# A hybrid decoder step on one core: the recurrence's pace, a later decode update, z through the weight landing buffers, and VectorE in order of tracing

## The chip, the cores and the metric

The kernel runs on one core of a Trainium2 chip. A core has five engines that work at the same time and meet through semaphores: TensorE (PE, matrix products), VectorE (DVE, elementwise work and reductions), ScalarE (ACT, functions and copies), GpSimd (POOL) and SyncE (SP, which issues most transfers). Each works through its own instructions in the order in which the program holds them. The metric is the time of one execution in microseconds on the device; lower is better.

## The reference

One inference step of two layers: a causal Conformer convolution and an RWKV-7 time-mixing layer, each followed by a squared-ReLU MLP, for 1040 prompt tokens (16 of them learned) and 8 decode rows, all in float32, width 1024, 16 heads of 64. The part that the change touches is the second layer's mixer and what follows it:

```python
def _wkv7_step(S, inp):
    r_t, w_t, k_t, v_t, kk_t, a_t = inp
    sa = jnp.einsum('bhvk,bhk->bhv', S, -kk_t)
    S = (S * w_t[:, :, None, :] + sa[..., None] * (kk_t * a_t)[:, :, None, :]
         + v_t[..., None] * k_t[:, :, None, :])
    y = jnp.einsum('bhvk,bhk->bhv', S, r_t)
    return S, y
...
    kk = kk / jnp.maximum(jnp.sqrt(jnp.sum(kk * kk, axis=-1, keepdims=True)), L2_EPS)
...
    S_final, ys = lax.scan(_wkv7_step, S0.astype(f32), xs)
...
    out = ((yn + bonus).astype(h.dtype) * g) @ w_o
...
def _sqrelu_mlp(h, w_in, w_out):
    return jnp.square(jax.nn.relu(h @ w_in)) @ w_out
```

The prompt's scan over 1040 tokens starts from zero; the 8 decode rows make one step from a given state.

## The kernel before

Everything is held with features on the 128 partitions and tokens along the free dimension. Products that need full accuracy are made of three fast ones: a weight block is split into a high part (ACT, L156) and a low part (POOL in four pieces, L161), the activations likewise (`split`, L137), and `mm3` (L186 to L188) adds up high*high, low*high and high*low.

**Stages.** The first layer runs to about 1120 us and isn't touched. Then come four mixer groups of 272, 256, 256 and 264 tokens (`mixer_in(g)`), then the output projection and the second MLP, first for the first third of the tokens (`mixer_out(0)` and `mlp`), then for the other two thirds together.

**Mixer group.** `prepare(g)` loads the input rows and makes differences and mixed inputs on DVE. `keys(g)` makes the eight key projections, keeps them, and sums their squares over heads in the PSUM tile `pn`; at its end stand the norm's reciprocal root `r16` and its split (L889 to L895). `mixer_in(g)` then goes through eight pairs of heads: projections r and v, the low-rank gate and decay, on DVE the normalised key (L1061, which needs `r16` through `spread`), a scan of the decay (L1062), and products into `ab`. `finish` of a pair is delayed by one pair: it writes `ab`, the transposed values and a block of products `n` to DRAM (L1009 to L1021). During pair p the keys of group g + 1 are made. The last pair's finish is `carry["tail"]`, run at the start of the next group, and behind the loop for the last one.

**Recurrence.** The scan is done in 17 chunks: chunk 0 of the 16 learned tokens, then 16 of 64. Per chunk the inverse of a triangular matrix is needed: `inverses` loads the blocks `n` of a group's four chunks back from DRAM (L1135) and eliminates row by row in 30 steps of two DVE operations (L1141, L1142), eight operations to a piece, and writes the result `d_p`. `front(c)` loads a chunk's operands and makes the products A, `chunk(c)` goes through the products gg, bT, W, po, U, S and Y, with a copy or an elementwise step on DVE or ACT between any two of them. Both are generators; each `yield` gives a weight from `RW` (sum 27.72), meant as the distance to the next step. `chunk` also calls `step(c + 1)` three times, which moves the next chunk's front on by one yield without its weight being charged; this happens only once that chunk's inverse is there.

**Ticks.** `tick(g)` is called at the start of a pair and twice within each projection: it moves the inverses by one yield, adds `PACE[g]` to a credit from which the recurrence's steps are paid (a credit that nothing could be paid from is lost), and moves the norms of the first token group (`ng0`: load y, head norms, write z to DRAM) by one yield. In the MLP, `filler` is called 208 times in the first group and spreads three streams over the calls in proportion: the rest of the recurrence, the decode rows' step (`decode_step`: eight transposes on PE, a round trip through DRAM, then 16 rounds of nine DVE operations on the state, L1375 to L1383) and the norms of the other tokens.

**Order.** A planner puts each engine's instructions in an order by its own simulation, priorities following the order of tracing. Within `in_order()` PE's instructions keep the order of tracing exactly; DVE, ACT, POOL and SP are the planner's. A tile's memory may be reused by tiles of a later pool; then each new tile waits for the old tiles that lie in its place. The pools of the mixers (input rows, differences, narrow weights, mixed inputs, low-rank tiles, pair tiles, in this order) are followed in the same place by those of the MLP: temporaries, statistics, activations, split weights, and so on.

**Output projection.** `mixer_out(g)` loads z through the temporaries `t1` (three buffers), splits it into `z`, and per block of 128 output features loads and splits the weights and multiplies (`dense`).

## Time and profile before

| | us |
|---|---|
| median of 3 runs | 2803.23 (2798.64 to 2806.42) |
| profiled execution, its own time | 2803.45 |
| its span, first to last instruction | 2801.7 |
| PE busy | 2654.4 (95%) |
| DVE busy | 1772.9 (63%) |
| POOL busy | 1497.7 (53%) |
| ACT busy | 1141.9 (41%) |

The span is read in stages: an engine's share of the whole span is a mean over stages with different limits. Busy times are read per window, waits by who released them, and the timeline instruction by instruction. In a timeline row stand start, duration, engine, line of the kernel, operation, output and inputs, count, and in brackets the idle time of that engine just before, with what ended it. PE's row of weight loads is called PEld; it runs beside the products.

### The profile page before, as it was taken

The numbers are of one execution on the slowest core, as the hardware profiler recorded it, in microseconds if no ns is written. First come the engines' busy times: TensorE is split into PE (matmuls) and PEld (weight loads), VectorE is DVE, ScalarE is ACT, GpSimd is POOL, SyncE is SP. The second block draws the span as 40 slices with busy tenths as digits, with TensorE's granted clock in tenths as the row PEclk, the third lists the DMA queues.
The fourth block names the chain that finished last, engine by engine and source line by source line (L and its number), as shares of the span: only waits on it lengthen the run. The fifth ranks groups of instructions, "written<-read, shape, count | busy, mean of one in ns | idle before, by whom it ended". The sixth has DMA issues, their size and how long they took to land. (4 is left out here: it accounts for less than half of the span.)

```text
span 2801.7 us, 51779 instructions
## 1 busy us (share of the span) xinstructions
PE 2654.4 (95%) x19866; PEld 2502.9 (89%) x19866; DVE 1772.9 (63%) x3550; ACT 1141.9 (41%) x2101; POOL 1497.7 (53%) x2066
## 2 busy tenths in 40 slices
PE   8998999999999999999998999978999999999998
PEld 7998999999999999787777778767889999999998
DVE  5999999996454544244756555589985554434444
ACT  5545444543354333233343443444444452222223
POOL 6676877887788866022111112366568763333332
PEclk9998999999999999999999999989999999999999
DMA  6663544454445553567778767877775642222211
GB/s 179 176 178 89 160 136 134 135 177 136 138 138 159 170 149 95 163 192 196 188 175 203 184 162 188 190 201 187 181 212 160 179 122 81 71 72 69 68 53 42
DMA packets 624599, 412.31 MB, mean 147 GB/s; under 512 B 121865, under 2 KB 567497, under 8 KB 624351
## 3 DMA queue, kind: packets, MB, share of 16 engines
q1 hardware_dynamic: 543436, 358.60, 45.1%
q10 hardware_dynamic: 72386, 24.56, 4.2%
q0 software_dynamic: 8528, 25.83, 2.8%
q8 instruction: 157, 2.57, 0.4%
q14 instruction: 92, 0.75, 0.1%
HBM read 345.76 MB, written 64.07 MB: 146 GB/s over the span
## 5 line engine op out<-in xcount | busy, mean ns | idle before, releaser
L161 POOL TENSOR_TENSOR wo_lo<-wo_raw,wo_hi 128x256 fp32r<-128x256 f32 x736 | 564.3, 798 | 261.0 <-ACT wo_hi L156 250.2
L161 POOL TENSOR_TENSOR wi_lo<-wi_raw,wi_hi 128x256 fp32r<-128x256 f32 x640 | 488.2, 794 | 282.7 <-ACT wi_hi L156 268.1
L186 PE MATMUL out<-hh,wo_hi 128*128 128x352 f32 (+2 forms) x1536 | 503.5, 328 | 21.5 <-DVE h L354 10.9
L354 DVE TENSOR_TENSOR h<-h,out 128x352 f32<-128x352 f32 (+2 forms) x768 | 387.5, 510 | 200.2 <-PE out L188 199.6
L188 PE MATMUL out<-hl,wo_hi 128*128 128x352 f32 (+2 forms) x1536 | 494.3, 324 | 5.5 <-DVE hl L140 5.5
L188 PE MATMUL ps_in<-m_l,wi_hi 128*128 128x352 f32 (+2 forms) x1536 | 495.5, 323 | 2.7 <-DVE m_l L284 2.6
L186 PE MATMUL ps_in<-m_h,wi_hi 128*128 128x352 f32 (+2 forms) x1536 | 496.4, 323 | 1.2 <-DVE h L354 1.2
L187 PE MATMUL out<-hh,wo_lo 128*128 128x352 f32 (+2 forms) x1536 | 495.8, 323 | 0.0
L187 PE MATMUL ps_in<-m_h,wi_lo 128*128 128x352 f32 (+2 forms) x1536 | 492.6, 321 | 0.0
L518 DVE SCALAR_TENSOR_TENSOR cv<-u,wdw,cv 128x352 f32<-128x352 f32 (+2 forms) x720 | 376.3, 571 | 0.7
L156 ACT CAST wi_hi<-wi_raw 128x1024 fp32r<-128x1024 f32 x160 | 168.0, 1050 | 399.9 <-PE out L188 195.8
L156 ACT CAST wo_hi<-wo_raw 128x1024 fp32r<-128x1024 f32 x184 | 192.6, 1049 | 320.0 <-PE out L188 159.0
L186 PEld LDWEIGHTS out<-hh,wo_hi 128*128 128x128 f32 x1536 | 293.1, 191 | 27.7 <-DVE h L354 13.2
L188 PEld LDWEIGHTS out<-hl,wo_hi 128*128 128x128 f32 x1536 | 291.1, 190 | 7.0 <-DVE hl L140 6.9
L186 PEld LDWEIGHTS ps_in<-m_h,wi_hi 128*128 128x128 f32 x1536 | 290.0, 189 | 3.9 <-issue 1.7
L187 PEld LDWEIGHTS out<-hh,wo_lo 128*128 128x128 f32 x1536 | 292.8, 191 | 0.6
L188 PEld LDWEIGHTS ps_in<-m_l,wi_hi 128*128 128x128 f32 x1536 | 288.6, 188 | 5.0 <-DVE m_l L284 4.1
L187 PEld LDWEIGHTS ps_in<-m_h,wi_lo 128*128 128x128 f32 x1536 | 289.4, 188 | 0.9
L341 DVE SCALAR_TENSOR_TENSOR r<-ps_in,rs_m 128x352 f32<-128x352 f32 (+2 forms) x192 | 98.3, 515 | 245.9 <-PE ps_in L188 240.7
L140 DVE TENSOR_TENSOR hl<-s,hh 128x352 fp32r<-128x352 f32 (+2 forms) x192 | 142.5, 743 | 104.6 <-ACT hh L139 104.4
L343 ACT ACTIVATE s<-r 128x352 f32<-128x352 f32 (+2 forms) x192 | 93.5, 490 | 121.9 <-DVE r L341 121.6
L1021 POOL DMA_DIRECT2D d_n<-n x32 | 24.4, 764 | 208.4 <-DVE n L1011 131.3
(354 smaller groups left out, 4855.9 us busy)
## 6 DMA issues: line engine op xcount, KB each, us to landing
wi_raw<-in_w_mlp_in_dram SPq DMA_DIRECT2D x160, 512.0 KB, 4.0
wo_raw<-in_w_mlp_out_dram SPq DMA_DIRECT2D x160, 512.0 KB, 3.8
wk_raw<-in_rwkv_w_k_dram SPq DMA_DIRECT2D x32, 512.0 KB, 7.2
wr_raw<-in_rwkv_w_r_dram SPq DMA_DIRECT2D x32, 512.0 KB, 4.2
wv_raw<-in_rwkv_w_v_dram SPq DMA_DIRECT2D x32, 512.0 KB, 4.5
d_ab<-ab POOLq DMA_DIRECT2D x32, 512.0 KB, 4.4
pg_raw<-in_conv_w_pw_dram SPq DMA_DIRECT2D x24, 512.0 KB, 6.8
pa_raw<-in_conv_w_pw_dram SPq DMA_DIRECT2D x24, 512.0 KB, 4.1
```

The source lines that it names most:

```text
L140: eng_lo.tensor_sub(lo, src, hi.bitcast(F32))
L156: nc.scalar.copy(hi[:, :a * b], raw[:, :a * b])
L161: eng_lo.tensor_sub(lo[:, cs], raw[:, cs], hi[:, cs].bitcast(F32))
L186: nc.tensor.matmul(ps, w[0], act[0], start=first, stop=False)
L187: nc.tensor.matmul(ps, w[1], act[0], start=False, stop=False)
L188: nc.tensor.matmul(ps, w[0], act[1], start=False, stop=last)
L341: nc.vector.scalar_tensor_tensor(r[:, :n], ps[:, :n], 0.0, rs()[:, :n], op0=ALU.max, op1=ALU.mult)
L343: nc.scalar.activation(s[:, :n], r[:, :n], AF.Square)
L354: nc.vector.tensor_add(hv[:, 4 * i + m, :], hv[:, 4 * i + m, :], ps[:, :n])
L518: nc.vector.scalar_tensor_tensor(acc[m][:, :n], ug[:, m, j:j + n], wdw[:, m, j:j + 1], acc[m][:, :n], op0=ALU.mult, op1=ALU.add)
L1021: nc.gpsimd.dma_start(d_n[ch0:ch0 + ncg, p].rearrange("c r t -> r c t"), n32[:, :ncg])
```

## The change

The change adds no arithmetic and removes none. It moves work in time, changes the order on DVE, and changes how z reaches the chip's memory.

- `PACE` goes from 2.0 in groups 1 to 3 to 1.4, 1.3 and 2.4, and four more ticks come behind the last group, ahead of its tail.
- Through the mixers DVE keeps the order of tracing too, as PE does. For this the last part of `keys` (the norm of the keys) becomes a step of its own, run behind the second tick of the next group, and the 32x32 transpose in `front` moves ahead of the products A.
- `decode_step` is put behind 74 empty units in its stream; the stream's length goes from 82 to 164.
- The split weights' pool of the MLP is opened ahead of the activations and the statistics, so that it lies in other old tiles.
- In `mixer_out`, z is loaded two or three feature blocks at a time into the weights' landing buffers (`raw`), and weight blocks are asked for two ahead.

```diff
@@ open_tmp @@
-        def open_tmp(stack, nmax, tag, bufs=3, **kw):
+        def open_tmp(stack, nmax, tag, bufs=3, stats=True, **kw):
...
+            if stats:
+                cur["stat"] = pool(stack, f"stat{tag}", 1, **kw)
@@ keys @@
                 add_pn()
                 add_pn = to_pn(p, sq)
+            yield
             r16 = lorap.tile([P, N1], F32, name=nm("r16"), tag="lf")
@@ mixer_in @@
-            r16p = norm.pop(g)
-            ks = iter(())
+            ks, kend = iter(()), carry["keys"]
+
+            def first():
+                both()
+                next(kend, None)
...
-                ps = proj(next(wrkv), act, n, nm("r", p), both)
+                ps = proj(next(wrkv), act, n, nm("r", p), both if p else first)
...
-                spread(pb[:, :n], r16p, p)
+                spread(pb[:, :n], norm[g], p)
...
-                        ks = keys(g + 1, both)
+                        ks = carry["keys"] = keys(g + 1, both)
@@ front @@
             yield RW[0]
+            x32 = w_([P, KT, 32], "x32", c)
+            nc.vector.transpose(flat(x32), flat(p32))
             mask = lambda x: m_ar[:, x].unsqueeze(1).broadcast_to([P, 4, HS])
...
-            x32 = w_([P, KT, 32], "x32", c)
-            nc.vector.transpose(flat(x32), flat(p32))
             chunks[c] = xa, bk, nr, no, p32, x32
@@ mixers @@
-        PACE = [0, 2.0, 2.0, 2.0]
+        PACE = [0, 1.4, 1.3, 2.4]
...
-        with in_order():
+        with tc.manual_schedule(engines={nc.tensor.engine, nc.vector.engine}):
             shift_in()
             for _ in prepare(0):
                 pass
-            for _ in keys(0, lambda: None):
-                pass
+            carry["keys"] = keys(0, lambda: None)
+            for _ in range(KT + 1):
+                next(carry["keys"])
             for g in range(4):
                 mixer_in(g, lambda slow=1.0: tick(g, slow))
+            for _ in range(4):
+                tick(3, 1.0)
             carry["tail"]()
@@ MLP pools @@
-            open_tmp(l1, N2, "2", 3)
+            open_tmp(l1, N2, "2", 3, False)
+            open_weights(l1, 0, {"w": 5}, "f")
             actp = pool(l1, "actp1", 1)
-            open_weights(l1, 0, {"w": 5}, "f")
+            cur["stat"] = pool(l1, "stat2", 1)
@@ mixer_out @@
+                block = lambda m: load_col(rwkv_w_o[0], m, f"wo{g}_{m}", nc.gpsimd)
                 z = new_acts(actp, f"z{g}", cur["wide"])
-                for p in range(KT):
-                    t = tt(f"zr{g}{p}", "t1")
-                    nc.sync.dma_start(t[:, :n], d_z[:, p, lo:lo + n])
-                    split(z[0][p][:, :n], z[1][p][:, :n], t[:, :n], nc.vector)
+                ws, per = [], 8 * P // n
+                for p in range(0, KT, per):
+                    t = cur["raw"].tile([P, 8 * P], F32, name=f"zr{g}{p}", tag="raw")
+                    some = min(per, KT - p)
+                    v = t[:, :some * n].rearrange("p (k t) -> p k t", k=some)
+                    nc.sync.dma_start(v, d_z[:, p:p + some, lo:lo + n])
+                    if p == 0:
+                        ws.append(block(0))
+                    for i in range(some):
+                        split(z[0][p + i][:, :n], z[1][p + i][:, :n], v[:, i], nc.vector)
+                ws.append(block(1))
                 for m in range(KT):
-                    ps = dense(load_col(rwkv_w_o[0], m, f"wo{g}_{m}", nc.gpsimd), z, n, f"oo{g}_{m}", fill)
+                    if m + 2 < KT:
+                        ws.append(block(m + 2))
+                    ps = dense(ws.pop(0), z, n, f"oo{g}_{m}", fill)
@@ MLP, first group @@
+            DL, DN = 74, 90
+
+            def late_start(n):
+                for _ in range(n):
+                    yield 1
...
-                                ([decode_step()], 82), ([norm_gates(GN_OF[1]), ng2], NGA))
+                                ([late_start(DL), decode_step()], DL + DN), ([norm_gates(GN_OF[1]), ng2], NGA))
```

More of the change, by code (lines that the diff above doesn't have):

```diff
@@ L121, in hybrid_step @@
         cur = {}
-        def open_tmp(stack, nmax, tag, bufs=3, **kw):
+        def open_tmp(stack, nmax, tag, bufs=3, stats=True, **kw):
             cur["n"] = cur["wide"] = nmax
             cur["tmp"] = pool(stack, f"tmp{tag}", bufs, **kw)
-            cur["stat"] = pool(stack, f"stat{tag}", 1, **kw)
+            if stats:
+                cur["stat"] = pool(stack, f"stat{tag}", 1, **kw)
         def stat(name, tag, bufs, w=None):
```

## The prediction

> **What bounds the kernel now.** I read the page first, for the stages.
>
> ```profile
> span 2801.7 us, 51779 instructions
> ...
> PE 2654.4 (95%) x19866; PEld 2502.9 (89%) x19866; DVE 1772.9 (63%) x3550; ACT 1141.9 (41%) x2101; POOL 1497.7 (53%) x2066
> ...
> DVE  5999999996454544244756555589985554434444
> ...
> PEclk9998999999999999999999999989999999999999
> ```
>
> TensorE (PE) is busy 95% of the span, but VectorE (DVE) has two regimes, and the granted clock dips where PE has gaps. The change touches the time from about 1130 to 2310 us, so I cut that in windows. Columns: window, length, then busy time (and instructions) of PE, weight loads, DVE, ScalarE (ACT), GpSimd (POOL), then clock, DMA share, GB/s. The four mixer groups are the first four rows, the hand-over to the last MLP is the fifth, that MLP's first group the next three, the start of its other two groups the last.
>
> ```profile
> 1130.00:1300.00 170.00, 165.91 (x975) 135.79 (x974) 60.87 (x143) 56.17 (x161) 34.12 (x67) 0.99 0.62 186
> 1300.00:1490.00 190.00, 174.53 (x1883) 144.79 (x1882) 111.91 (x282) 73.63 (x186) 30.03 (x50) 0.96 0.77 188
> 1490.00:1690.00 200.00, 182.07 (x2080) 149.78 (x2078) 115.08 (x265) 85.03 (x207) 29.04 (x48) 0.97 0.73 185
> 1690.00:1820.00 130.00, 125.54 (x1282) 103.85 (x1282) 70.60 (x172) 52.47 (x144) 36.29 (x79) 0.99 0.76 186
> 1820.00:1840.00 20.00, 10.82 (x144) 8.41 (x145) 10.55 (x23) 9.94 (x20) 10.49 (x18) 0.71 0.84 272
> 1840.00:1900.00 60.00, 47.16 (x506) 43.27 (x499) 56.69 (x103) 26.21 (x51) 40.36 (x51) 0.91 0.68 177
> 1900.00:2070.00 170.00, 151.80 (x1849) 141.64 (x1847) 159.80 (x325) 73.44 (x142) 97.51 (x108) 0.95 0.70 177
> 2070.00:2206.00 136.00, 132.44 (x877) 130.88 (x875) 71.92 (x133) 59.02 (x87) 110.82 (x146) 1.00 0.60 186
> 2206.00:2310.00 104.00, 99.99 (x601) 97.11 (x602) 64.48 (x91) 57.26 (x107) 73.92 (x91) 0.98 0.51 151
> ```
>
> PE idles 4.1 + 15.5 + 17.9 + 4.5 = 42.0 us in the mixers, 9.2 in the hand-over, 12.8 + 18.2 = 31.0 in the front of the MLP's first group, 3.6 in its back and 4.0 after it: 89.8 us. A clock below 1 costs busy time times the shortfall: mixers 1.7 + 7.0 + 5.5 + 1.3 = 15.5 us, hand-over 3.1, front 4.2 + 7.6 = 11.8. That is all there is to win: some 120 us. DVE is busy 94% of both front windows (56.7 of 60, 159.8 of 170) and 53% of the back (71.9 of 136): in the front PE waits for DVE, in the back it waits for nothing. The list of what PE waited for from 1834 to 2070 says the same:
>
> ```profile
> PE bT L1244 <- DVE nr L1186: 9.1, 7, 3.2
> ...
> PE ps_oo L186 <- ACT wo_hi L156: 5.8, 1, 5.8
> ...
> PE S L1276 <- ACT uv L1269: 4.9, 1, 4.9
> ```
>
> **The change part by part.** The sum is made against the profiled execution's own time, 2803.45 us (span 2801.7), which is 0.2 us from the median 2803.23.
>
> *Hand-over.* The timeline between the last mixer and the output projection:
>
> ```profile
> 1822.39 0.38 PE L992 MATMUL vt<-ident,vv 128*128 128x128 f32 x2
> ...
> 1827.48 0.46 PE L1009 MATMUL nn<-ab 64*32 64x32 f32 x32 [3.21 <-DVE ab L1093]
> ...
> 1832.69 0.83 ACT L139 CAST z_h<-zr 128x328 fp32r<-128x328 f32 x2 [2.86 <-DMA zr<-d_z]
> ...
> 1833.42 4.83 ACT L156 CAST wo_hi<-wo_raw 128x1024 fp32r<-128x1024 f32 x5
> ...
> 1834.52 0.64 PE L186 MATMUL ps_oo<-z_h,wo_hi 128*128 128x328 f32 x1 [5.79 <-ACT wo_hi L156]
> ```
>
> PE's last projection ends about 1822.4; it then has a value transpose, a wait of 3.2 us for the last pair's operands, and 5.8 us for the first weight block, which ACT cast only behind the z casts (they waited for loads going through three small buffers). The changed code loads z in 3 transfers instead of 8, traces block 0 ahead of the z casts, and puts the split weights where tiles lie that are free early in the last group (the input rows, their differences, the narrow weights), so the 5.8 us go. Four more ticks at 2.4 units put recurrence work in the 3.2 us. In SP's queue the z loads now stand ahead of weight block 1; they wait only for the first group's norms, which by the pace below are through by some tick 16 of 44. z_h waits for the memory of the last mixed inputs, so not all of 9.2 + 3.1 goes: bounds 3 and 11, I take **-7**.
>
> *Pace.* A tick gives credit; a chunk charges 27.72, but three steps of the next chunk's front (4 + 2.4 + 3.12 = 9.52) run uncharged once its inverses are there, so 18.2. At 2.0 flat, 56 ticks a group (40 in the last), the recurrence outruns the inverses (ready at tick 16, in group 1 at 23) and stops. Its DVE copies show how far it gets, 11 of 17 chunks in the mixers and 6 after:
>
> ```profile
> 1160.00:1820.00 660.00, 7.44 (x11) 0.98 0.72 185
> 1834.00:2206.00 372.00, 4.03 (x6) 0.96 0.66 183
> ```
>
> At 1.4, 1.3, 2.4 with 44 last ticks it gets 67, 73, 106 units: group 1 ends within chunk 2, group 2 within chunk 6, group 3 finishes chunk 12. So 13 in the mixers, 4 after; their PE time changes place and cancels. Steps lie 1.4 to 1.5 times as far apart in groups 1 and 2, which hold 33.4 of the 42.0 us of idle time; in group 3 they come closer (2.4 for 2.0), and in all of them recurrence now runs beside the inverses, where it used to stand.
>
> *VectorE in order of tracing.* No instruction is added; DVE may no longer run something ahead of one that waits. The last step of the keys is traced behind the next group's second tick, and so behind the first piece of the inverses, which waits for a round trip through DRAM. Group 3's start now:
>
> ```profile
> 1693.47 1.28 ACT L893 ACT_TABLE_LOAD   x1
> ...
> 1694.26 0.43 DVE L892 TENSOR_SCALAR r<-pn 128x264 f32<-128x264 f32 x1 [3.70 <-PE pn L879]
> ...
> 1697.51 0.43 DVE L140 TENSOR_TENSOR r16l<-r,r16h 128x264 fp32r<-128x264 f32 x1 [0.48 <-ACT r16h L139]
> ...
> 1703.66 0.29 DVE L1011 TENSOR_TENSOR n<-nn,nmask 128x128 f32<-128x128 f32 x1 [5.72 <-PE nn L1009]
> ...
> 1713.43 0.20 DVE L1141 TENSOR_TENSOR tt<-ni 128x30 f32<-128x30 f32 x1 [8.76 <-DMA ni<-d_n]
> ...
> 1721.31 0.48 PE L755 MATMUL pb<-r16h,hspread 128*128 128x264 f32 x1
> ```
>
> The inverse starts 9.8 us after its last input is made (1703.66 to 1713.43). The key norm takes 3.7 us (1694.26 to 1697.94) plus a table load of 1.28, today ahead of all this. Placed behind the first six inverse operations of some 0.2 us (to about 1714.7) it ends at 1719.7; PE wants it at 1721.3. Covered by 1.6 us; without the cover each us late is a us of PE in three groups. The scan now stands behind that product as well, but its result is wanted a whole pair later. The x32 transpose goes ahead of the products it used to follow: nothing. Pace and order together: at best they halve idle and clock loss in the mixers (57.5 / 2 = -29), at worst they add as much as group 2 idles today (+18). Nearer to a small gain, since the spacing helps the two groups that idle most: **-6**.
>
> *Decode later.* Its transposes are on PE, in order, so they hold it back truly: from call 74/164 of 208 on; its state update runs from (74 + 18)/164 = 56% to 95% of the stage. Today it lies wholly in the window 1900 to 2070. First row: its operations that touch the temporary; second: the one that doesn't; third: one operation's minimum, median, maximum in ns.
>
> ```profile
> 1900.00:2070.00 170.00, 66.04 (x127) 0.95 0.70 177
> ...
> 1900.00:2070.00 170.00, 9.16 (x16) 0.95 0.70 177
> ...
> L1375 DVE TENSOR_TENSOR t<-Sdec,dq x16: 406/462/959, 1919.0 to 2065.0; 128x256 f32<-128x256 f32 x16
> ```
>
> That is 66.0 + 9.2 = 75.2 us of DVE taken out of a window in which it is busy 159.8 of 170, and put in one where it is busy 71.9 of 136. 71.9 + 75.2 = 147.1 overfills the back by 11.1 us. The front keeps the last inverses:
>
> ```profile
> L1142 DVE TENSOR_TENSOR ni<-ni,tt 128x30 f32<-128x30 f32 (+14 forms) x30 | 17.3, 578 | 0.7
> ...
> L1141 DVE TENSOR_TENSOR tt<-ni 128x30 f32<-128x30 f32 (+14 forms) x30 | 16.9, 564 | 3.5 <-DMA ni<-d_n 2.8
> ```
>
> 34.2 us there, unmoved. Progress of the MLP's matmuls (one of three equal lines):
>
> ```profile
> 1834.00:2063.00 229.00, 84.37 (x264) 51.46 (x264) 0.94 0.70 180
> 2063.00:2110.00 47.00, 27.39 (x87) 16.77 (x88) 0.96 0.85 259
> 2110.00:2206.00 96.00, 65.44 (x210) 39.34 (x210) 1.00 0.49 151
> ```
>
> Today the recurrence ends with 264 of 561 done, 47%. The changed one ends at 85 units of 166 = 51%. So the window 1900 to 2070 loses both the decode and two chunks, and I count two thirds of its idle and clock loss (18.2 + 7.6) as won, 17; of the window with the inverses (12.8 + 4.2) a quarter, 4; against that 7 of the 11.1 us overflow, since some decode runs ahead into gaps. **-14**; bounds +5 and -30.
>
> The decode operations take 572 ns in the mean (9.16 / 16), and a like one 406 at best, 959 at worst: something slows them. The Trainium skill (page "SBUF — State Buffer", section "Who interferes with whom") has it that a DVE instruction with two SBUF inputs contends with a GpSimd instruction that reads SBUF, for a port pair held for a whole instruction. It speaks against this edit: POOL is busy 57% of the front window (97.5 of 170) and 81% of the back (110.8 of 136). By that rule the excess of 166 ns would grow with POOL's share by 70 ns, as an estimate, for 7 x 16 operations 8 us in the back; the term would be -6 and the time 2782, inside the forecast's own range. No run here shows it yet.
>
> *Landing buffers for groups 1 and 2.*
>
> ```profile
> zr<-d_z SPq DMA_DIRECT2D x16, 176.0 KB, 3.7
> ```
>
> 16 transfers of 176 KB become 8 of 352 KB, and weights are asked for two blocks ahead. The window 2206 to 2310 idles 4.0 us: bounds 0 and -4, taken **-2**.
>
> Sum: -7 - 6 - 14 - 2 = -29; 2803.45 - 29 = **2774.5 us**.
>
> **The rivals.**
> *B, PE becomes the only bound.* If pacing and order clear the mixers too: -11 there, -29 in the mixers, -30 in the MLP, -4 after: -74 at most, I put it at -60, **2743**. For it: DVE, the next engine, is busy 722 of these 1180 us, 61%. Against it: the inverse chain (below) is left in every group.
> *C, the back of the MLP becomes bound by DVE.* The whole overflow is paid and the mixers win nothing: -7 + 0 + 0 - 2, about **2795**. For it: 147.1 us of work in 136. Against it: that is DVE's load today in the front.
> *D, the in-order DVE queue blocks PE at each group's start (slower).* The inverses' DVE time in the mixers:
>
> ```profile
> L1141 DVE TENSOR_TENSOR tt<-ni 128x30 f32<-128x30 f32 (+21 forms) x104 | 33.7, 324 | 26.2 <-DMA ni<-d_n 23.7
> ...
> L1142 DVE TENSOR_TENSOR ni<-ni,tt 128x30 f32<-128x30 f32 (+21 forms) x104 | 33.6, 323 | 2.7
> ```
>
> 67.3 us, 22.4 a group, in pieces of eight operations, one piece a tick. In order of tracing, a recurrence product that PE waits for stands behind a piece, and the first piece behind the DRAM round trip. It decides once more than 29 of 67 us (43%) reach PE; at 70%, +47 - 29 = +18: **2821**. For it: recurrence now runs during the inverses, and the last group has the shortest ticks. Against it: steps are 1.28 to 5 units apart, 1 to 4 ticks in group 2, so a piece of some 3 us is mostly over by then.
> *E, it does not do what it says.* The planner orders ACT, POOL and SP itself; if it puts the weight cast behind the z casts again and DVE's stalls only change their place, **2800**.
>
> **How the numbers follow.** A 0.50 (own range 2758 to 2790), B 0.17, C 0.16, D 0.12, E 0.05. A measurement of this kernel tells 0.3% (8.4 us) from no change: 2794.8 to 2811.6. Faster: A, B, 0.06 of C, 0.02 of E = 0.75; same 0.09 of C, 0.02 of E = 0.11; slower D, 0.01 of C, 0.01 of E = 0.14. The range from 2745 to 2806 leaves out half of B and D, 0.2.
>
> **What would show it.** Hand-over: the first output-projection matmul within some 9 us of the last v projection (12.1 now), with no wait for the weight cast. Pace: 13 copies of the U product before the MLP, 4 after. Decode: none of its updates before the middle of the stage, DVE below 85% in the front, above 95% in the back. Order: no wait of PE for the key norm above 2 us at a group's start, and PE idle in groups 1 and 2 below today's 33.4 us. The prediction is wrong if PE idles over 60 us in the mixers (D), or if the back of the MLP's first group takes over 150 us for the same matmuls (C).

## The result, and the profile after

The changed kernel takes 2825.61 us (median of 4 runs, 2819.31 to 2828.16), the kernel before 2804.12 (4 runs, 2798.64 to 2806.42): ratio 1.0082, 95% interval 1.0065 to 1.01, slower by 0.8%. The forecast was 2774.5, faster, with a range from 2745 to 2806. The profiled execution is the quickest of the four: its own time is 2819.31 and its span 2817.6, so its rows account for 16 of the 22 us.

Windows of the changed kernel, columns as in the windows before the change: window, length, busy time of PE, weight loads, DVE, ACT, POOL, then clock, DMA share, GB/s. The cuts follow the stages, which now end later: four mixer groups, the hand-over, three parts of the MLP's first group, the start of its other groups.

```profile
1130.00:1300.00 170.00, 169.98 (x1039) 141.15 (x1038) 57.87 (x146) 58.02 (x162) 32.99 (x64) 1.00 0.64 191
1300.00:1490.00 190.00, 169.49 (x1646) 141.97 (x1645) 104.26 (x273) 68.34 (x174) 26.73 (x47) 0.95 0.73 194
1490.00:1690.00 200.00, 179.07 (x1976) 150.60 (x1976) 109.51 (x253) 80.27 (x197) 28.89 (x49) 0.94 0.71 172
1690.00:1830.00 140.00, 127.51 (x1739) 105.64 (x1738) 85.01 (x200) 62.16 (x168) 39.73 (x82) 0.96 0.70 171
1830.00:1860.00 30.00, 13.29 (x176) 10.61 (x174) 13.59 (x27) 11.71 (x25) 21.40 (x28) 0.66 0.89 240
1860.00:1920.00 60.00, 38.51 (x418) 36.61 (x415) 45.48 (x96) 20.10 (x36) 28.45 (x34) 0.83 0.61 154
1920.00:2090.00 170.00, 162.85 (x1818) 154.70 (x1817) 109.01 (x199) 84.08 (x160) 100.80 (x128) 0.98 0.69 184
2090.00:2222.00 132.00, 117.78 (x751) 112.53 (x750) 126.31 (x253) 51.15 (x76) 104.41 (x124) 1.00 0.57 168
2222.00:2326.00 104.00, 99.82 (x603) 97.70 (x604) 61.83 (x90) 57.23 (x104) 76.52 (x95) 0.95 0.56 158
```

PE idles 20.5 + 20.9 + 12.5 us in mixer groups 1 to 3 (15.5 + 17.9 + 4.5 before; group 0, 4.1 before, has none left), 16.7 in the hand-over (9.2), 21.5 right behind it (12.8), 7.2 in the rest of the front (18.2) and 14.2 in the back (3.6). So group 0 and the rest of the front did improve; the mixers as a whole (53.9, 42.0 before), the hand-over, the time right behind it and the back got worse. The waits of PE, first from 1300 to 1860, then from 1860 to 1935, then from 2100 to 2235 (in all, times, longest):

```profile
PE ps_oo L187 <- ACT z_h L140: 14.0, 1, 14.0
PE l_w L957 <- ACT lw L947: 13.4, 2, 8.3
PE S L1281 <- ACT uv L1274: 11.9, 1, 11.9
PE Y L1288 <- DVE nr L1193: 6.6, 1, 6.6
...
PE gg L1231 <- DVE x L1177: 18.4, 1, 18.4
...
PE out L187 <- DVE r L342: 8.9, 7, 1.8
PE out L187 <- ACT hh L140: 6.4, 1, 6.4
```

*The queue in the mixers.* VectorE's timeline in group 2, around the 11.9 us:

```profile
1500.92 0.20 DVE L1442 RECIPROCAL ems<-ems 128x8 f32<-128x8 f32 x1 [4.90 <-ACT ems L1441]
...
1509.71 0.68 DVE L1098 TENSOR_TENSOR ab<-wa,em 128x512 f32<-128x512 f32 x1
...
1512.58 3.32 DVE L839 SCALAR_TENSOR_TENSOR mx<-xx,pvec,hx 128x264 f32<-128x264 f32 x8
1515.83 0.40 DVE L1146 TENSOR_TENSOR tt<-ni 128x240 f32<-128x240 f32 x1
1516.26 0.41 DVE L1147 TENSOR_TENSOR ni<-ni,tt 128x240 f32<-128x240 f32 x1
...
1526.55 0.19 DVE L1147 TENSOR_TENSOR ni<-ni,tt 128x30 f32<-128x30 f32 x1
1526.66 0.68 DVE L1273 COPY uv<-U 64x512 f32<-64x512 f32 x1
1527.26 0.43 DVE L1177 STREAM_TRANSPOSE x<-p 128x256 f32<-128x256 f32 x1
```

PE's S begins at 1528.00 after 11.9 us of nothing, that is, it was free at 1516.1. It needs U copied in two halves: VectorE's takes 0.68 us and runs at 1526.66, and ScalarE's, the one named in the list of waits, follows at 1527.37. VectorE's half stands behind 30 inverse operations with no other work between them (1515.83 to 1526.74). From 1501 on VectorE doesn't idle; in the pile it works on what nobody is waiting for yet. Just ahead of the cut, in its fixed order, it had stood 4.9 us for ScalarE's root in a norm of the first token group (L1442), so part of its lateness at this place is a wait. A kernel below with a quarter of the inverses (n1) keeps such waits and loses only 1.3 us in the mixers.

*The hand-over.* ScalarE ahead of the first output matmul (1854.3):

```profile
1842.22 1.04 ACT L157 CAST wo_hi<-wo_raw 128x1024 fp32r<-128x1024 f32 x1 [3.81 <-DMA wo_raw<-in_rwkv_w_o_dram]
...
1846.34 1.04 ACT L157 CAST wo_hi<-wo_raw 128x1024 fp32r<-128x1024 f32 x1 [2.31 <-DMA wo_raw<-in_rwkv_w_o_dram]
1852.88 1.04 ACT L157 CAST wo_hi<-wo_raw 128x1024 fp32r<-128x1024 f32 x1 [5.50 <-DMA wo_raw<-in_rwkv_w_o_dram]
1853.83 3.03 ACT L140 CAST z_h<-zr 128x328 fp32r<-128x328 f32 x8
```

Before, the cast of block 0 stood behind the z casts; now the z casts stand behind those of several later blocks, each of which waits for a load.

*The last inverse.* U's copies, up to the output projection and behind it: 12 and 5 (11 and 6 before, 13 and 4 in the forecast).

```profile
1160.00:1850.00 690.00, 8.17 (x12) 0.95 0.70 183
1850.00:2222.00 372.00, 3.37 (x5) 0.95 0.64 176
```

The first chunk behind the hand-over is the last whose inverse is ready. The next needs the last group's inverses; their last step, the load of the stored result and what follows it, from the timelines:

```profile
1903.79 0.65 DVE L1147 TENSOR_TENSOR ni<-ni,tt 128x30 f32<-128x30 f32 x1
...
1910.62 0.99 SPq L1174 DMA_DIRECT2D p<-d_p  x2
...
1913.35 0.45 DVE L1177 STREAM_TRANSPOSE x<-p 128x256 f32<-128x256 f32 x1 [8.92 <-DMA p<-d_p]
...
1913.95 1.06 PE L1231 MATMUL gg<-x,no 32*32 32x32 f32 x32 [18.40 <-DVE x L1177]
```

Before, one chunk more was left to fill that time.

### The profile page after: what moved, and what is told of

The parts are those of the page before. It is cut to its first block, busy times and chain, and to the rows that moved or that the text cites. A ratio compares the mean times of both kernels' runs of the same rounds, so it can differ in the third digit from the quotient of the medians.

```text
span 2817.6 us, 51679 instructions
## 1 busy us (share of the span) xinstructions
PE 2644.4 (94%) x19866; PEld 2499.0 (89%) x19866; DVE 1766.1 (63%) x3550; ACT 1143.1 (41%) x2099; POOL 1497.9 (53%) x2066
```

## The experiments

All times are medians; "before" was run beside each. To see where a difference sits, the table cuts the profiled executions at PE's products with the key norm (`pb`, once a pair): *mixers* is from the first to the last of them, *hand* from there to the first output matmul, *MLP* from there to the first output matmul of the second token group. One execution's stage lengths carry some us of their own: the first `pb` stands at 1182.5 us in the changed kernel's profile and at 1189.6 before (1181.7 to 1190.5 in all kernels of the table), and behind the third stage the changed kernel takes 581.2 us, 585.7 before. So its three stages are 27.7 us longer together, and its profiled execution 15.9.

| kernel | us | ratio to before (95%) | mixers | hand | MLP |
|---|---|---|---|---|---|
| before | 2804.1 | 1 | 633.8 | 11.1 | 381.4 |
| changed | 2825.6 | 1.0082 (1.0065, 1.01) | 645.3 | 26.6 | 382.1 |
| a1, VectorE free | 2790.0 | 0.9955 (0.9942, 0.9968) | 612.5 | 15.9 | 385.9 |
| a2, decode early | 2825.0 | 1.0078 (1.0064, 1.0092) | 647.7 | 26.6 | 383.1 |
| a3, old loading | 2821.3 | 1.0068 (1.0054, 1.0082) | 644.9 | 19.8 | 383.2 |
| a4, old pace | 2812.9 | 1.0037 (1.0023, 1.0051) | 647.0 | 15.9 | 378.9 |
| m1, key norm first | 2822.6 | 1.0063 (1.0049, 1.0076) | 642.6 | 26.8 | 381.6 |
| m2, piece later | 2840.9 | 1.0134 (1.0121, 1.0147) | 661.9 | 26.0 | 381.7 |
| m3, order in pairs 3-7 | 2795.1 | 0.9969 (0.9957, 0.9981) | 613.7 | 25.4 | 382.3 |
| m4, order in pairs 0-2 | 2817.9 | 1.0053 (1.0037, 1.007) | 641.2 | 16.1 | 388.0 |
| m5, recurrence first | 2828.1 | 1.0086 (1.0073, 1.0098) | 646.2 | 26.4 | 382.3 |
| n1, quarter, ordered | 2771.4 | 0.988 (0.9865, 0.9895) | 617.0 | 26.3 | 360.2 |
| n2, quarter, free | 2768.4 | 0.9875 (0.9859, 0.9891) | 615.7 | 15.9 | 369.4 |
| p1, inverses on POOL | 2809.0 | 1.0016 (1.0004, 1.0028) | 633.1 | 26.0 | 379.0 |
| d1, decode late alone | 2799.4 | 0.9985 (0.9974, 0.9997) | 637.5 | 11.4 | 380.5 |
| f1, free, old pace | 2793.3 | 0.996 (0.9947, 0.9972) | 627.4 | 14.7 | 374.8 |
| f2, free, last pace 1.85 | 2783.4 | 0.9921 (0.9906, 0.9937) | 617.7 | 20.3 | 376.1 |
| f3, f2 with old loading | 2777.0 | 0.991 (0.989, 0.993) | 609.4 | 14.7 | 377.9 |
| b1, f3, decode from 37 | 2781.0 | 0.9915 (0.9902, 0.9927) | 610.8 | 15.1 | 381.9 |
| p2, f3, inverses on POOL | 2789.3 | 0.9946 (0.9934, 0.9958) | 623.2 | 15.6 | 378.7 |

### Each part taken back

a1:

```diff
-        with tc.manual_schedule(engines={nc.tensor.engine, nc.vector.engine}):
+        with in_order():
             shift_in()
```

> The changed kernel, with only TensorE in the order of tracing (VectorE is free again). Theory 1: the idle time of TensorE at the starts of mixer groups 1 to 3 comes from VectorE's fixed order (the U product's copy behind 25 inverse operations, the key norm behind the first inverse piece), so the mixers' idle falls from 54 us to 30 or less, and the time from 2825.6 to about 2805. Rival: the pace makes these stalls, since recurrence now runs beside the inverses; then the mixers keep some 50 us of idle and the time stays within 5 us of 2825.

2790.0: 35.6 us off, and faster than the kernel before. With the other parts as changed, the order is more than the whole loss. The mixers lose 32.8 us of length and the hand-over 10.7; PE's list of waits from 1300 to 1820 no longer has the U copy or the product mask in front:

```profile
PE l_w L957 <- ACT lw L947: 4.9, 1, 4.9
PE pb L756 <- ACT vv L1059: 4.4, 2, 4.2
...
PE ps_oo L187 <- ACT z_h L140: 2.0, 1, 2.0
```

VectorE's timeline at the same chunk shows how the planner does it:

```profile
1504.44 0.39 DVE L1147 TENSOR_TENSOR ni<-ni,tt 128x238 f32<-128x238 f32 x1
1504.76 0.41 DVE L1086 TENSOR_TENSOR wa<-rk,wa 128x256 f32<-128x256 f32 x1
...
1508.14 0.39 DVE L1147 TENSOR_TENSOR ni<-ni,tt 128x240 f32<-128x240 f32 x1
1508.46 0.67 DVE L1273 COPY uv<-U 64x512 f32<-64x512 f32 x1
```

One inverse operation at a time between the pair's own work, and the U copy among them as soon as U is there.

a2:

```diff
-                                ([late_start(DL), decode_step()], DL + DN), ...
+                                ([decode_step()], 82), ...
```

> The changed kernel, with the decode state update spread from the start of the last MLP's first group again. Theory C: the late decode fills VectorE in the back of that group and costs the 14 us that TensorE idles there (3.6 before); early decode gives 10 us back and finds room in the front, so about 2815. Rival (my forecast's reason): the front is where VectorE is the bound, so the 75 us of decode cost more there than they save in the back: 2830 to 2840.

No difference (0.6 us). Neither theory's size. The front stands for the last inverse anyway (13.9 us in this kernel, 18.4 in the changed one), so early decode has room there; that would explain it, but wasn't tried by itself.

a3: `mixer_out` and the pools as before (one z tile at a time through `t1`, one weight block at a time, `actp` ahead of the weights).

```diff
-                ws, per = [], 8 * P // n
-                for p in range(0, KT, per):
...
-                ws.append(block(1))
                 for m in range(KT):
-                    ps = dense(ws.pop(0), z, n, f"oo{g}_{m}", fill)
+                    ps = dense(load_col(rwkv_w_o[0], m, f"wo{g}_{m}", nc.gpsimd), z, n, f"oo{g}_{m}", fill)
```

> The changed kernel, with the output projection's inputs through the three small buffers, weights asked for one block at a time, and the pools in the old order. Theory: ScalarE now has four weight casts ahead of the cast that the first matmul needs (14.0 us of wait), which is dearer than the 5.8 us before; the old loading gives about 7 us back: 2818. Rival: the hand-over is set by the release of memory by the last mixer, and the wait only changes its name: within 3 us of 2825. Forecast's reason: 2830 to 2835.

4.3 us less in the medians, though the two intervals overlap; in the profiled executions the hand-over is 6.8 us shorter. It points to the theory's side.

a4:

```diff
-        PACE = [0, 1.4, 1.3, 2.4]
+        PACE = [0, 2.0, 2.0, 2.0]
...
-            for _ in range(4):
-                tick(3, 1.0)
```

> The changed kernel, with the recurrence at 2.0 units a tick in every group and without the four ticks at the end of the last. Theory: the even pace leaves no chunk whose inverse is ready for the time in which the last group's inverses run, which is the 18.4 us wait of TensorE for the transposed rows of a chunk; with chunks 11 and 12 left for that time the wait goes below 5 us and the time falls by 10 to 18 us, to about 2811. Rival: the pace helps the mixers by what it costs there; then the time stays within 5 us of 2825, and the idle only moves into groups 1 and 2.

12.7 us less, as the theory had it: the wait of `gg` is gone from PE's list, while the mixers stay as long as they were (647.0 and 645.3). Under the order, the new pace wins nothing in the mixers.

### What in the order costs

m1 and m2:

```diff
                     for _ in keys_of(p):
                         next(ks, None)
+                    if p == KT - 1:
+                        next(ks, None)
```
```diff
-            yield 5
+            for _ in range(4):
+                yield 5
...
-            for _ in range(3 if c == 0 else 7):
+            for _ in range(3 if c == 0 else 4):
```

> The changed kernel, VectorE in order, but with the key norm of the next group traced at the end of the last pair again, ahead of the first inverse piece. Theory 1a: part of the 35.6 us that the fixed order costs (2825.6 to 2790.0) is the key norm behind the first piece: it delays ScalarE and so the 8.3 and 5.1 us waits for the cast lw at the starts of groups 1 and 2; without it 2812 to 2817. Rival 1b: what blocks VectorE is the inverses alone, whatever stands behind them; then within 4 us of 2825.

> The changed kernel, VectorE in order, with the first inverse piece traced three ticks later and the inverses still called ready at the same tick. Theory 1b: VectorE stands in the first piece until the round trip through DRAM is over (6.5 us at group 1, 8.8 before the change), and all that is traced behind it comes late; with the piece traced when its data has landed, the mixers lose some 15 to 25 us: 2800 to 2810. Rival 1c: it is the mass of inverse work (22 us a group) in front of what TensorE waits for, not the round trip: within 5 us of 2825, or later inverses make it worse by some us at the last group.

m1 brings 3 us, not told apart from nothing: the key norm is not it, though its own wait (`l_w`) shrinks from 13.4 to 3.3 us. m2 takes away VectorE's idle time for the inverses' loads (10.4 us in the changed kernel's mixers, none in m2) and yet costs 15.3 us: it isn't the round trip through DRAM. PE now waits longest for the gates (`l_w`, 16.5) and for the copy of W (12.6). That pieces which come later hold up what is then urgent would explain it; it wasn't followed further.

m3 and m4 put VectorE's order on parts of each group, and leave VectorE free elsewhere:

```diff
-            both = lambda: tick(1.0)
+            both, dv = lambda: tick(1.0), ExitStack()
...
             for p in range(KT):
-                both()
+                both() if p != 3 else (dv.enter_context(tc.manual_schedule(engines={nc.vector.engine})), both())
...
+            dv.close()
...
-        with tc.manual_schedule(engines={nc.tensor.engine, nc.vector.engine}):
+        with in_order():
```

and m4 the other way round, entered ahead of the gates and closed at pair 3.

> VectorE in the order of tracing only from pair 3 to pair 7 of each mixer group, that is behind the ticks in which the inverses of the group before are traced; free in the gates and in pairs 0 to 2. The rest as changed. Theory 1c: the fixed order costs 35.6 us because the inverses (22 us of VectorE a group) then stand in one queue with the copies and products that TensorE waits for; without order beside them nothing is lost: 2788 to 2796. Rival 1d: order costs all along a group, in proportion to the instructions under it (5 of 8 pairs, some 22 us): 2808 to 2815.

> VectorE in the order of tracing only in the gates and pairs 0 to 2 of each mixer group, where the inverses are traced; free from pair 3 on. The rest as changed. Theory 1c: this holds the whole cost, 2818 to 2828. Rival 1d: in proportion (3 of 8 pairs, some 13 us): 2800 to 2806.

The first three pairs, in which the inverses are traced, carry 27.9 of the 35.6 us, the five others 5.1, whose interval overlaps that of no order at all; in m3 the mixers are as short as in a1, and what is longer is the hand-over (25.4, 15.9 in a1). PE's waits in m4 from 1300 to 1830 are those of the changed kernel, the U copy's to the tenth:

```profile
PE S L1281 <- ACT uv L1274: 11.9, 1, 11.9
PE l_w L957 <- ACT lw L947: 10.2, 2, 7.8
PE Y L1288 <- DVE nr L1193: 6.5, 1, 6.5
```

Those pairs hold more than inverses, so n1 and n2 leave out 22 of the 30 elimination steps of each inverse, with the order and without; what they compute is not the reference's result:

```diff
+                if j % 4 == 0 or j == 1:
...
-                nc.vector.tensor_mul(o, ...)
-                nc.vector.tensor_add(ni[:, :j, j + 1:top], ni[:, :j, j + 1:top], o)
+                    nc.vector.tensor_mul(o, ...)
+                    nc.vector.tensor_add(ni[:, :j, j + 1:top], ni[:, :j, j + 1:top], o)
```

> The changed kernel, VectorE in order, with 8 of the 30 elimination steps of each inverse kept (so the inverses, and what the recurrence makes of them, are not the reference's); ticks, pieces and transfers stay. To be read beside the next kernel. Theory 1c: it is the inverses' VectorE time that blocks the queue; with about a quarter of it the order costs 10 us or less, not 35.6: 2785 to 2800 here. Rival 1e: the order costs by the instructions that share pairs 0 to 2, inverses or not: 25 to 35 us more than the next kernel, 2810 to 2820.

> VectorE free, 8 of the 30 elimination steps of each inverse kept (inverses not the reference's), the rest as changed. The inverses' time is then no load on VectorE, and the wait of TensorE for the last inverse (16.0 us) gets shorter by some 10 to 14: 2774 to 2782, beside 2790.0 with all steps.

2771.4 and 2768.4: with a quarter of the inverses the order costs 3 us, and the intervals overlap; the mixers differ by 1.3 us, not 32.8. (The hand-over is still 10.4 us longer with the order, and the MLP 9.2 shorter.) In n1 the U copy still stands behind the inverse operations, but there are 8 of them, done in 2.6 us:

```profile
1504.02 0.39 DVE L1147 TENSOR_TENSOR tt<-ni 128x228 f32<-128x228 f32 x1
...
1506.48 0.19 DVE L1148 TENSOR_TENSOR ni<-ni,tt 128x30 f32<-128x30 f32 x1
1506.59 0.68 DVE L1274 COPY uv<-U 64x512 f32<-64x512 f32 x1
```

n2 also went below its expectation of 2774 to 2782: its MLP stage is 16.5 us shorter than a1's. m5 asks which inverses stand in front:

```diff
-            invert()
             advance(PACE[g] * slow, NCH - 1)
+            invert()
```

> The changed kernel, VectorE in order, with the recurrence traced ahead of the inverse piece in each tick. Theory 1c with the piece of the same tick as what stands in front: a piece of some 3 us leaves the way of each step, 2805 to 2815. Theory 1c with the pile of earlier pieces (VectorE a pair behind TensorE): little changes, 2820 to 2826.

2828.1, no gain. It is not the piece of the same tick but what was traced in earlier ones: PE's longest wait in the mixers is now U's, 11.5 us for the copy of W (at 1524.33), ahead of which VectorE does 24 inverse operations (1495.7 to 1506.9) and stands 5.6 us for the root of a norm.

p1 keeps all the work and moves it off the queue:

```diff
-            top = META if c == 0 else 32
+            top, eng = META if c == 0 else 32, nc.gpsimd if c < 13 else nc.vector
...
-                nc.vector.tensor_mul(o, ...)
+                eng.tensor_mul(o, ...)
```

> The changed kernel, VectorE in order, with the elimination steps of the inverses of groups 0 to 2 (those traced in the mixers) on GpSimd. Theory 1c: with the inverses out of VectorE's queue, the order costs next to nothing, as with a quarter of the steps: some 2790, what the kernel with VectorE free takes, if GpSimd (busy 130 of the mixers' 690 us) does them in time. Rival 1f: what counts is when an inverse is ready; a slower engine makes the recurrence wait and GpSimd's queue (the stores of each pair's operands) stand behind the pieces: 2815 or more.

2809.0, between the two: 16.6 us less than the changed kernel, and not the 2790 of theory 1c. The same move with VectorE free (p2, below) costs 12.3 us; if it costs as much here, the slower engine is most of what is missing.

### The parts alone, and a faster kernel

d1 is the kernel before with `late_start` and the new weight of the decode stream (the diff's lines, and nothing else).

> The kernel before with the late decode alone. Theory: VectorE was the bound in the front of the last MLP's first group (32.4 us of idle on TensorE in front of 2100, against 17.9 with late decode, old pace and VectorE free), and the back pays 10 for it: 2796 to 2800. My forecast's -14: 2789. Rival: in the changed kernel the place of the decode made no difference (2825.6 and 2825.0), so none here: 2801 to 2806.

4.3 us less, the weak end of the theory, ratio 0.9985 (0.9974 to 0.9997). Its windows beside those of the kernel before (1900 to 2070 and 2070 to 2206):

```profile
1900.00:2070.00 170.00, 164.49 (x1979) 154.28 (x1980) 111.76 (x209) 83.20 (x163) 100.01 (x124) 1.00 0.75 190
2070.00:2206.00 136.00, 121.04 (x761) 115.33 (x760) 127.18 (x252) 51.71 (x74) 110.91 (x131) 0.99 0.59 176
```

The front wins 12.7 us of PE time (151.8 to 164.5) and full clock; the back loses 11.4 (132.4 to 121.0) at a VectorE that is 94% busy; PE waits most there for VectorE's step of the MLP's activation (`out` for `r`, L341: 8.4 us in 7 waits).

f1 is a1 with a4's edit.

> VectorE free, and the recurrence at 2.0 units a tick without the four last ticks; decode, landing buffers as changed. Before is 2803.4, VectorE free with the new pace 2790.0. Theory 2: with VectorE free the even pace is worth some 15 to 20 us in the mixers (633.8 us from the first to the last key-norm product before, 612.5 with the new pace), and gives 10 back in the wait for the last inverses: 2797 to 2802. Rival: the pace only changes where the recurrence runs, and the wait for the last inverses (16.0 us) is a pure loss: 2775 to 2785.

2793.3 against 2790.0, not told apart: the new pace shortens the mixers by 14.9 us, with a chunk more in them, and lengthens the MLP by 11.1. So f2 takes a1 and lowers only the last pace:

```diff
-        PACE = [0, 1.4, 1.3, 2.4]
+        PACE = [0, 1.4, 1.3, 1.85]
```

> VectorE free, paces 1.4, 1.3 and 1.85 in the last group (2.4 in the changed kernel), so that about one chunk more is left for the time of the last inverses. Theory 3: the wait of TensorE for the transposed rows of the first chunk of the last group (16.0 us) falls below 6 and the time with it, to about 2780. Rival: the chunk taken out of the last mixer group is missed there, or fills the front of the MLP where VectorE is the bound: 2788 to 2795.

2783.4, a gain of 6.6 over a1; the wait for the last inverse (16.0) is gone from the list, and the hand-over's (16.1) is now the longest. f3 is f2 with a3's edit:

> VectorE free, paces 1.4, 1.3, 1.85, and the output projection's inputs through the three small buffers with the pools in the old order. Theory: in the kernel with these paces and the new loading (2783.4) the first output matmul waits 16.1 us for its input's cast, behind four weight casts on ScalarE; the old order casts the inputs first, so about 8 us less there and some 2 us more in the two later groups: 2776 to 2780. Rival: as with the changed kernel, where the old loading brought 4.3 us, 2779, or nothing, 2783.

2777.0, ratio 0.991 (0.989 to 0.993), faster than the kernel before by 0.9%; from f2 the intervals don't tell it apart. Its longest wait is again the one of the kernel before, for the weight cast, now 10.5 us:

```profile
PE ps_oo L187 <- ACT wo_hi L157: 10.5, 1, 10.5
PE Y L1288 <- DVE nr L1193: 4.8, 2, 2.6
```

b1 changes `DL` from 74 to 37 in f3, p2 moves its inverses to GpSimd:

> VectorE free, paces 1.4, 1.3, 1.85, old loading of the output projection's inputs (2777.0), with the decode's state update from call 37 of its stream on and not 74. Theory: TensorE idles 11.2 us in the back of the last MLP's first group because the decode is squeezed into its second half, and 22.4 in the front; spread over 70% of the stage the back gives up to 6 us back: 2771 to 2777. Rival: what the back gains the front loses: 2777 to 2782.

> VectorE free, paces 1.4, 1.3, 1.85, old loading of the output projection's inputs (2777.0), with the inverses of groups 0 to 2 on GpSimd. Theory: with VectorE free the inverses fit into its gaps, so nothing is won: 2773 to 2779. Rival 1f: GpSimd is slower at them and its queue holds up stores: 2785 or more.

2781.0, not told apart from f3: in the profiled executions the front loses 7.4 us of PE time (231.3 to 224.0, 1835 to 2080) and the back gains 3.5 (100.2 to 103.7, 2080 to 2193). 2789.3: GpSimd is slower at this, as the rival said. Neither helps, and f3 has the lowest median of the kernels that do all the work.

## Why the forecast was wrong, point by point

Along one path the runs add up: decode, loading and the moved key norm and transpose together -10.3 (f1 against its own run of before), the pace -3.3 (f1 to a1), VectorE's order +35.6 (a1 to the changed kernel), in all +22.0; side by side it was +21.5. The parts of f1 were not all tried alone: decode is -4.3 of it (d1). The split between order and pace depends on the path: with the old pace the order costs 19.6 (f1 to a4), and the new pace under the order another 12.7 (a4 to the changed kernel). The sum is 32.3 either way; some 16 us of it arise only where the two come together.

*The step that failed* is in the term "pace and order together", taken as -6 with bounds of -29 and +18; it measured +32.3. The forecast let "a piece of some 3 us" stand in front of a recurrence product, "mostly over by then" because steps lie 1 to 4 ticks apart, and so gave rival D 0.12. In the trace no single piece stands in front but the pile: 30 operations, the last four of a group's eight pieces, in a row. The step that failed is to price one piece at a time, and not all that VectorE has been given by then. Why it piles up follows from numbers that the forecast had. An estimate: some 22 us of inverses are traced in 8 ticks, little more than one pair, beside that pair's own VectorE work of some 11 us (group 2 has 109.5 us of it, less 22, over 8 pairs). That is some 33 us of VectorE's work in about a pair, and a pair of PE lasts 16 to 21 us where VectorE is free (the first three of group 2 in a1; 13.1, 36.6 and 18.2 in the changed kernel, the second with the wait shown above). VectorE, kept to this order, falls behind, and what is traced after is late. VectorE free does the same inverses in gaps between the pair's other work.

D's account (more than 43% of 67 us would have to reach PE) held: 35.6 of 67.3 is 53%. D was the mechanism; that its time, 2821, is so near to 2825.6 is luck. Its price for the order was too high (47, measured 35.6), and what it set against it too large (29, measured 13.6 along the path above). Its 47 also lies outside the +18 that the forecast's own term allowed. Its sign, PE idle over 60 us in the mixers, stayed out: 53.9. The loss there is in the clock as well: busy time times the shortfall is 24.3 us in the changed kernel's windows, 15.5 before.

*The key norm* was the place at which the forecast looked ("covered by 1.6 us"). It isn't covered, and the wait comes earlier than at the product that it looked at. At group 1's start:

```profile
1304.90 0.17 DVE L1146 TENSOR_TENSOR tt<-ni 32x14 f32<-32x14 f32 x1 [6.49 <-DMA ni<-d_n]
...
1306.05 0.41 DVE L894 TENSOR_SCALAR r<-pn 128x256 f32<-128x256 f32 x1
...
1314.60 0.38 ACT L947 ACTIVATE lw<-p_wa 64x256 f32<-64x256 f32 x1
...
1315.03 1.22 PE L957 MATMUL l_w<-lw,wa 128*128 128x256 f32 x2 [8.28 <-ACT lw L947]
```

VectorE stands 6.5 us in the first piece for its load, as D had it, the norm comes behind, and ScalarE does the norm's root and split ahead of the function `lw` that the gates need. Putting the norm back takes most of this wait away and still gives only some 3 us (m1), since VectorE stays late further on (S waits the same 11.9 us for the copy of U in m1).

*The pace.* The spacing is worth what was hoped where VectorE is free (mixers 14.9 us shorter, f1 to a1) and nothing under the order (a4). What the forecast didn't have at all: by its sum it counted the moved chunks as "changes place and cancels", but the chunks left for the MLP are work that PE does while the last inverses run. With one fewer, `gg` waits 18.4 us. In the copies of U it was also off by one (12 and 5).

*The hand-over*, -7 taken, measured 15.5 us longer. Rival E had the reason, the planner's order on ScalarE, but the other way round: it puts the z casts behind the weights. Five weight casts run between 1830 and 1854, and the last three wait for loads. The same code waits from 2.0 us (a1) to 16.1 (f2), so what decides is when those loads get through, not the buffers. The new loading by itself accounts for 4.3 (a3) to 6.4 us (f2 to f3), neither told apart by its interval. By the table the rest goes with order and pace together: the hand-over takes 25.4 to 26.8 us in each kernel with the new loading, the new pace and VectorE in order over the last pairs, and some 16 without that order (a1, m4, n2) or with the old pace (a4); but f2, with VectorE free, takes 20.3. Why the loads are late in one kernel and not in another stays open.

*Decode later*, -14 taken, is right in its mechanism and too large: alone -4.3. The front won what was counted (idle and clock of 1900 to 2070: 12.7 us more PE time). The back was mis-sized: the overflow of 11.1 was priced at 7, and PE already loses 11.4 there with VectorE at 94%, before it is full. Part of it is that the decode's own operations take longer there: 84.7 us in d1, 75.6 before (the last section). The forecast's sum left them as long as they were. In the changed kernel VectorE's load moves as forecast (167.7 of 246 us in the front, 118.7 of 122 in the back, from the rows below) and the move is worth nothing (a2), perhaps because the front stands still for the last inverse.

```profile
1854.00:2100.00 246.00, 217.01 (x2333) 205.84 (x2334) 167.74 (x318) 114.37 (x216) 142.78 (x177) 0.93 0.68 182
2100.00:2222.00 122.00, 107.78 (x684) 102.54 (x682) 118.70 (x239) 43.83 (x62) 94.46 (x112) 1.00 0.55 164
```

*The landing buffers* for the two later groups, -2 taken, can't be seen in the window at their start (4.2 us idle, 4.0 before). From the second group's first output matmul to the end of the execution, the 14 kernels with the new loading take 581.1 to 584.4 us, 582.3 in the mean, and the 6 with the old 582.7 to 585.7, 583.8 in the mean: some 1.5 us less, near to what was taken, with ranges that overlap.

## What to carry to other kernels

An engine's fixed order is only as good as the rate at which work is traced into it: before fixing one, sum for each short stretch of the trace what is put into that engine's queue, urgent or not, and compare it with the time of the engine that sets the pace; a long background chain traced in a burst must be kept out of the order (m3), or perhaps spread over the whole stage, which wasn't tried here. And ask what the order is to bring: in no pair of kernels here did VectorE in order take less time than VectorE free. Before work is moved ahead to fill one stage, look for the wait that it was covering in the next. And an engine that takes work off a full one starts to be the bound well below 100% where the consumer needs its results one by one (here at 94%).

## What the runs showed of the hardware that was not expected

The 104 elimination steps in the mixers (two operations each) take 33.7 and 33.6 us on VectorE in the kernel before, by the rows at rival D. The same count on GpSimd, in p1, from 1290 to 1830 (first the products, then the sums; columns window, length, DVE, POOL):

```profile
1290.00:1830.00 540.00, 0.00 (x0) 56.14 (x104) 0.96 0.74 184
...
1290.00:1830.00 540.00, 0.00 (x0) 55.70 (x104) 0.96 0.74 184
```

By the profile that is 1.7 times as long, and still the kernel with VectorE in order gained 16.6 us by it.

The decode's nine operations a round are the same in every kernel, and the change moves them to a place where GpSimd has more to do. Seven of them read two inputs in SBUF, the on-chip memory; the other two are reductions of one input. Busy time of all 16 rounds, and GpSimd's share of the time from the first to the last of them:

| kernel | GpSimd busy | seven operations with two inputs (112), us | two reductions (32), us |
|---|---|---|---|
| before | 84.3 of 148 us, 57% | 62.4 | 13.2 |
| a2, decode early | 83.7 of 147 us, 57% | 64.4 | 13.1 |
| changed | 92.3 of 114 us, 81% | 71.3 | 13.2 |
| d1, decode late alone | 92.9 of 115 us, 81% | 71.5 | 13.2 |

The seven take 8.8 us longer in the changed kernel than before (79 ns each) and 9.1 in d1 (81 ns each), the reductions no longer. Where nothing but the decode's place differs, it is 6.9 (a2 and the changed kernel) and 9.1 (before and d1). The row that the forecast weighed (Sdec<-Sdec,dq) goes from 572 to 627 ns; one of the seven goes the other way (t<-Sdec,dq, from 594 to 541).

By the Trainium skill (page "SBUF — State Buffer", section "Who interferes with whom") a DVE instruction with two SBUF inputs contends with a GpSimd one that reads SBUF. The forecast's estimate by that rule, 70 ns an operation and 8 us in all, agrees with these rows. With it the forecast's term would have been -6, nearer to d1's -4.3 than the -14 that it took. That GpSimd's reads are the reason isn't shown by them: no run here had POOL idle beside the decode.
